# Stick-breaking attention: the causal mask of a diagonal block made by the running product

## The chip, the cores and the metric

The kernel runs on one core of one Trainium2 chip. The time is device microseconds of one execution, from three executions before the change. A core has five engines that run at the same time, each in the order of its own instructions: PE (matrix products; a product and the load of its stationary operand are two instructions), DVE (vector work), ACT (activations and copies), POOL (further vector work) and SP, which here only issues DMAs. Semaphores between them make one wait for another.

## What is computed

A decoder block over 2048 tokens of width 1024: a normalised and modulated input is projected to q, k, v (8 heads of 64) and to 4 pooling groups; attention and pooling are projected back, and a SwiGLU feed-forward of width 2816 follows. The part that matters is the attention. It is strictly causal, and the weight of key s for query t is a product of sigmoids:

```python
z = jnp.einsum('bhqd,bhkd->bhqk', qb, kb) * inv_sqrt
mask = s_idx < t_idx
log1m = jnp.where(mask, -jax.nn.softplus(z), 0.0)
after = lax.cumsum(log1m, axis=3, reverse=True) - log1m
logw = jax.nn.log_sigmoid(z) + after
w = jnp.where(mask, jnp.exp(jnp.where(mask, logw, 0.0)), 0.0)
outs.append(jnp.einsum('bhqk,bhkd->bhqd', w, vb))
```

So w[t, s] = sigmoid(z[t, s]) times the product over all s < j < t of sigmoid(-z[t, j]), and 0 for s >= t.

## The kernel before

The program has three stages: the projections (up to some 320 us), the attention (some 320 to 845 us), into which the rest of the projections is woven in small pieces, and the output projection with the feed-forward. In the first two the order of PE, ACT, DVE and POOL is the order in which the code is written; the order of SP's DMAs is set by a scheduler.

The attention works head by head. Tokens come in 4 blocks of 512 (`tb` for queries, `sc` for keys). A unit (`h, tb, sc`) is one block of queries against one block of keys, `sc` from `tb` down to 0, so the first unit of each `tb` is the diagonal one; 8 heads have 80 units, 32 of them diagonal. A unit is 4 steps, one for each 128 queries (`i`). A diagonal step needs only the first L = (i+1)*128 keys, any other all 512. There are 320 steps, 128 of them diagonal. The loop at L960 issues for each step, in this order:

- `values_step` (L844): two products with the values for an earlier step; they add up in the one output bank `av`, which ACT copies out (L858) when a block of queries is through.
- `weights_step` (L794): two products q*k (L803, L804), high and low half of q, into one of two score banks. In a diagonal step a third product (L806), identity times `neg_r`, adds -1e30 to the last 128 columns wherever the key is not before the query. Then ACT makes `sg` = sigmoid(z/8) (L808) and `pr` = sigmoid(-z/8) (L810).
- `scan_step` (L813), one step later: DVE's running product along `pr`, from the last key to the first (L821). It starts from 1 (`one`) in a diagonal unit and from the carry of the block to the right otherwise. The scan takes a second operand, which the operation `bypass` ignores: a bank of zeros, `idle` (L892). POOL sets the column after the last key to the start value (L818 or L820), keeps the carry (L825) and makes w = sg * pr shifted by one (L827).
- `turn_step` (L830), 7 steps later: four transposes of w on PE (L838), then the rounded copy `wth` on ACT (L59) and the rest `wtl` on DVE (L60), for `values_step`.
- pieces of the remaining projections: per piece three products (L69 to L71).

With -1e30 in z the masked `sg` are 0 and the masked `pr` are 1, so they add nothing and leave the running product alone. Keys, queries and values of a block are loaded by SP (L785 to L787) when their buffers come free; SP also stores the attention output (L860) and the pooled means (L389).

The constants of this part are made at the start: `ident_r` on DVE, `neg32` on POOL, `neg_r` on DVE (L159 to L171), `idle` just before the first attention step (L893).

Of the kernel before, what the change touches and what calls it, by code (L numbers as in the profile page):

```python
# [9 lines left out]
F32 = mybir.dt.float32  # L10
F32R = mybir.dt.float32r
AF = mybir.ActivationFunctionType
ALU = mybir.AluOpType
# [4 lines left out]
P = 128  # L18
# [10 lines left out]
TB = 512  # L29
NTB = S // TB  # L30
NT = S // P
EPS = 1e-6
NEG = -1e30
LAG = 2
OFF = 7
PRB = 6
# [8 lines left out]
def block_kernel(ctx, tc, x, c, w_cond, b_cond, g_mix_pre, g_mix_post, w_in, w_pool,  # L45
                 pool_scale, w_out, g_ffn_pre, g_ffn_post, w_gate, w_up, w_down, out):
    nc = tc.nc
# [25 lines left out]
    def open_pool(stack, name, bufs=1, side=None):  # L73
        kw = {"side": side} if side else {}
        return stack.enter_context(tc.tile_pool(name=name, bufs=bufs, reuse_waits="tile", **kw))
# [22 lines left out]
    ident = const.tile([P, P], F32, tag="ident", name="ident")  # L98
# [41 lines left out]
    c1 = open_pool(ph1, "c1")  # L140
# [3 lines left out]
    def psum(tag, bufs, name):  # L144
        return psp.tile([P, TB], F32, tag=tag, bufs=bufs, name=name)
# [7 lines left out]
    def bank_cycle(*tags):  # L153
        tags = itertools.cycle(tags)
        return lambda name: psum(next(tags), 1, name)

    z_ps, t_ps, av_ps, mm_only = bank_cycle("z0", "z1", "z2"), bank_cycle("w0", "w1"), bank_cycle("a0", "a1"), bank_cycle("mm")

    ident_r = c1.tile([P, P], F32R, tag="ident_r", name="ident_r")  # L159
    nc.vector.tensor_copy(ident_r, ident)  # L160
    ones = c1.tile([P, P], F32, tag="ones", name="ones")
    nc.vector.memset(ones, 1.0)
    one = ones[:, 0:1]
    ones_r = c1.tile([P, P], F32R, tag="ones_r", name="ones_r")
    nc.vector.tensor_copy(ones_r, ones)
    neg32 = c1.tile([P, P], F32, tag="neg32", name="neg32")
    nc.gpsimd.memset(neg32, 0.0)
    nc.gpsimd.affine_select(out=neg32, in_=neg32, compare_op=ALU.is_gt, fill=NEG, base=0,
                            pattern=[[-1, P]], channel_multiplier=1)
    neg_r = c1.tile([P, P], F32R, tag="neg_r", name="neg_r")  # L170
    nc.vector.tensor_copy(neg_r, neg32)  # L171
    rcnt = c1.tile([P, 16], F32, tag="rcnt", name="rcnt")
    for j in range(16):
        nc.gpsimd.memset(rcnt[:, j:j + 1], 1.0 / (j + 1))
# [239 lines left out]
    base = {"q": 0, "k": SBW, "u": 3 * SBW}  # L414
# [379 lines left out]
    def weights_step(u, i):  # L794

        h, tb, sc = u
        diag = sc == tb
        kt, qt = kv[h, sc][0], qts[h, tb]
        L = (i + 1) * P if diag else TB
        nm = f"{h}_{tb}_{sc}_{i}"  # L800
        z = z_ps(f"z{nm}")
        keys = kt[:, 0:L]
        nc.tensor.matmul(z[:, 0:L], qt[:, 0, i * P:(i + 1) * P], keys, start=True, stop=False)  # L803
        nc.tensor.matmul(z[:, 0:L], qt[:, 1, i * P:(i + 1) * P], keys, start=False, stop=not diag)  # L804
        if diag:
            nc.tensor.matmul(z[:, i * P:L], ident_r, neg_r, start=False, stop=True)  # L806
        sg = att.tile([P, TB], F32, tag="sg", bufs=5, name=f"sg{nm}")
        nc.scalar.activation(sg[:, 0:L], z[:, 0:L], AF.Sigmoid, scale=0.125)  # L808
        pr = att.tile([P, TB + 1], F32, tag="pr", bufs=PRB, name=f"pr{nm}")
        nc.scalar.activation(pr[:, 0:L], z[:, 0:L], AF.Sigmoid, scale=-0.125)  # L810
        scans.append((u, i, pr, sg, L, nm))

    def scan_step(u, i, pr, sg, L, nm):  # L813

        diag = u[1] == u[2]
        carry = carries.pop(i, None)
        if carry is None:
            nc.gpsimd.memset(pr[:, L:L + 1], 1.0)  # L818
        else:
            nc.gpsimd.tensor_copy(pr[:, L:L + 1], carry)  # L820
        nc.vector.tensor_tensor_scan(pr[:, 0:L][:, ::-1], pr[:, 0:L][:, ::-1], idle[:, 0:L],  # L821
                                     one if carry is None else carry, ALU.mult, ALU.bypass)
        if u[2]:
            carries[i] = att.tile([P, 1], F32, tag=f"carry{i}", bufs=2, name=f"carry{nm}")
            nc.gpsimd.tensor_copy(carries[i], pr[:, 0:1])  # L825
        w = att.tile([P, TB], F32, tag="w", bufs=OFF + 4, name=f"w{nm}")
        nc.gpsimd.tensor_tensor(w[:, 0:L], sg[:, 0:L], pr[:, 1:L + 1], ALU.mult)  # L827
        wss.setdefault(u, []).append(w)
# [43 lines left out]
    def fillers():  # L872
        yield from pieces(1, chunks, tasks, [first_filler])
        while small or urgent:
            run_small()
            yield
# [3 lines left out]
    fill = fillers()  # L880
# [8 lines left out]
        next(fill)  # L889
    taken = START  # L890
    attending = True
    idle = psum("z2", 1, "idle")  # L892
    nc.vector.memset(idle, 0.0)  # L893
    z_ps, t_ps, av_ps, mm_only = bank_cycle(*('z0', 'z1')), bank_cycle(*('w0', 'w1', 'a1')), bank_cycle(*('a0',)), bank_cycle(*('mm',))
    steps = [(u, i) for u in units for i in range(4)]

# [63 lines left out]
    for n in range(len(steps) + OFF):  # L960
        if len(waiting) > LAG:
            values_step(*waiting.pop(0))
        if n < len(steps):
            u, i = steps[n]
            if i == 0:
                unit_loads(u)
            weights_step(u, i)
            spent += 2.5 if u[1] == u[2] else 4.0
        if len(scans) > 1 or n >= len(steps) and scans:
            scan_step(*scans.pop(0))  # L970
# [4 lines left out]
        while fill is not None and taken < goal:  # L975
            taken += 1
            if next(fill, 0) == 0:
                fill = None
# [607 lines left out]
```

## Time and profile before

| | |
|---|---|
| median of 3 executions | 2335.81 us (2334.72 to 2337.44) |
| span of the profiled execution, first to last instruction | 2331.9 us |
| median time less that span | 3.9 us |
| instructions in the profile | 33384 |
| granted TensorE clock, mean | 0.992 |
| HBM read, written | 274.51 MB, 128.45 MB |

The profile gives busy time for each engine, the chain of work that ended last, groups of equal instructions, waits between engines, and the instructions in order of time. An instruction shows its source line, engine, operation, and out<-in by the program's names. PE's products overlap and their ends are modelled: how long PE is taken by one is read from the start of the next, not from its duration. Times of the profiled execution are set against its span; the 3.9 us around it are not part of the profile.

### The profile page before, as it was taken

How to read it: one execution, taken by the hardware profiler on the slowest of the kernel's cores; microseconds unless marked ns; L12 is line 12 of the kernel's file. 1: busy time of each engine (PE TensorE's matmuls, PEld its weight loads, DVE VectorE, ACT ScalarE, POOL GpSimd, SP SyncE). 2: the span in 40 equal slices, each digit the busy share in tenths (PEclk: the TensorE clock that was granted, in tenths of full speed). 3: DMA queues.
4: the chain of work that ended last, by engine and by line, in shares of the span. 5: the costliest groups of instructions: out<-in, count | busy, mean ns of one | idle time of the engine just before them, and what ended most of it. 6: DMA issues, size and time to landing. Idle time of an engine off the chain costs nothing.

```text
span 2331.9 us, 33384 instructions
## 1 busy us (share of the span) xinstructions
PE 2265.3 (97%) x10717; PEld 1861.7 (80%) x10717; DVE 1633.5 (70%) x2222; ACT 1165.0 (50%) x2411; POOL 1316.0 (56%) x1621
## 2 busy tenths in 40 slices
PE   6999999999999999999999999999999999999997
PEld 3777888788888778887888888788888888888885
DVE  6774559999999966756666665887766556565556
ACT  4323658889989854444323232554533323234444
POOL 4542347787778854555687878331486665641004
PEclk9999999999999999999999999999999999999998
DMA  8785764333435536655545455776753333328554
GB/s 287 258 293 186 289 179 116 110 100 94 124 105 152 166 105 207 215 196 177 172 154 160 156 158 185 266 244 217 256 177 117 110 113 91 113 90 281 193 194 145
DMA packets 307116, 405.17 MB, mean 174 GB/s; under 512 B 19254, under 2 KB 179578, under 8 KB 303868
## 3 DMA queue, kind: packets, MB, share of 16 engines
q1 hardware_dynamic: 302620, 400.68, 53.1%
q10 hardware_dynamic: 4320, 2.36, 0.4%
q8 instruction: 84, 1.38, 0.2%
q14 instruction: 92, 0.75, 0.1%
HBM read 274.51 MB, written 128.45 MB: 173 GB/s over the span
## 4 chain that ended last, share of the span: by engine, by line
PE 80%; DVE 5%; POOL 5%; issue 4%; DMA 3%; ACT 3%; SPq 1%; POOLq 0%; DVEq 0%; ACTq 0%
PE wt L838 4%; PE t_u L71 3%; PE t_u L69 3%; PE t_u L70 3%; PE t_g L70 3%; PE t_g L69 3%; PE t_g L71 3%; PE dn0p L70 3%; PE dn0p L71 3%; PE dn0p L69 3%; PE dn1p L70 3%; PE dn1p L69 3%; PE dn1p L71 3%; PE av L853 3%; PE av L854 2%
## 5 line engine op out<-in xcount | busy, mean ns | idle before, releaser
L827 POOL TENSOR_TENSOR w<-sg,pr 128x512 f32<-128x512 f32 (+2 forms) x320 | 307.3, 960 | 41.9 <-DVE pr L821 22.3
L1186 POOL TENSOR_TENSOR s<-s,cu 128x512 f32<-128x512 f32 x88 | 133.6, 1525 | 239.5 <-DVE cu L1185 130.9
L821 DVE TENSOR_TENSOR_SCAN pr<-pr,carry,idle 128x512 f32<-128x512 f32 x192 | 243.8, 1270 | 0.0
L808 ACT ACTIVATE sg<-z 128x512 f32<-128x512 f32 (+2 forms) x320 | 181.3, 567 | 56.4 <-PE z L806 25.8
L60 DVE TENSOR_TENSOR wtl<-wt,wth 128x512 fp32r<-128x512 f32 (+1 forms) x320 | 189.2, 592 | 27.0 <-ACT wth L59 25.2
L59 ACT CAST wth<-wt 128x512 fp32r<-128x512 f32 (+1 forms) x320 | 180.8, 566 | 12.7 <-PE wt L838 12.7
L810 ACT ACTIVATE pr<-z 128x512 f32<-128x512 f32 (+2 forms) x320 | 180.8, 565 | 0.0
L838 PE MATMUL wt<-ident,w 128*128 128x128 f32 x1088 | 173.7, 274 | 3.7 <-POOL w L827 1.9
L60 DVE TENSOR_TENSOR u_s_l<-u_s,u_s_h 128x512 fp32r<-128x512 f32 x66 | 67.3, 1020 | 153.1 <-ACT u_s_h L59 153.1
L838 PEld LDWEIGHTS wt<-ident,w 128*128 128x128 f32 x1088 | 129.3, 141 | 31.0 <-POOL w L827 2.6
L1176 ACT ACTIVATE s<-s 128x512 f32<-128x512 f32 x88 | 55.7, 633 | 192.9 <-DVE s L1175 192.9
L853 PE MATMUL av<-wth,vt 128*128 128x512 f32 (+1 forms) x320 | 129.3, 404 | 5.8 <-ACT o L858 5.8
L70 PE MATMUL dn0p<-w0p_l,g0p_h 128*128 128x512 f32 x308 | 121.1, 393 | 0.9 <-DVE w0p_l L60 0.9
L69 PE MATMUL dn0p<-w0p_h,g0p_h 128*128 128x512 f32 x308 | 120.5, 391 | 0.0
L71 PE MATMUL dn0p<-w0p_h,g0p_l 128*128 128x512 f32 x308 | 120.4, 391 | 0.0
L854 PE MATMUL av<-wtl,vt 128*128 128x512 f32 (+1 forms) x320 | 118.8, 371 | 1.6 <-DVE wtl L60 1.3
L803 PE MATMUL z<-kt,qt 128*128 128x512 f32 (+2 forms) x320 | 117.9, 368 | 2.1 <-ACT pr L810 1.3
L59 ACT CAST g_s_h<-g_s 128x512 fp32r<-128x512 f32 x66 | 39.5, 620 | 159.3 <-POOL g_s L1118 83.2
L60 DVE TENSOR_TENSOR u_a_l<-u,u_a_h 128x512 fp32r<-128x512 f32 x66 | 75.9, 1151 | 61.1 <-ACT u_a_h L59 61.1
L804 PE MATMUL z<-kt,qt 128*128 128x512 f32 (+2 forms) x320 | 117.1, 366 | 0.0
L59 ACT CAST u_s_h<-u_s 128x512 fp32r<-128x512 f32 x66 | 38.6, 614 | 153.2 <-POOL u_s L1118 153.2
L70 PE MATMUL dn1p<-w1p_l,g1p_h 128*128 128x512 f32 x292 | 114.4, 392 | 0.0
(656 smaller groups left out, 7297.3 us busy)
## 6 DMA issues: line engine op xcount, KB each, us to landing
g<-in_w_gate_dram SPq DMA_DIRECT2D x42, 512.0 KB, 4.7
u<-in_w_up_dram SPq DMA_DIRECT2D x42, 512.0 KB, 4.7
wc<-in_w_cond_dram SPq DMA_DIRECT2D x32, 512.0 KB, 5.8
qt<-qd SPq DMA_DIRECT2D x64, 256.0 KB, 3.9
wd<-in_w_down_dram SPq DMA_DIRECT2D x44, 256.0 KB, 2.9
tdt<-wd SPq DMA_DIRECT2D x44, 256.0 KB, 2.0
w0p<-tdt SPq DMA_DIRECT2D x44, 256.0 KB, 4.2
w1p<-tdt SPq DMA_DIRECT2D x44, 256.0 KB, 2.7
```

What stands on the lines that cost most here:

```text
L59: nc.scalar.copy(hi, src)
L60: low.tensor_tensor(lo, src, raw(hi), ALU.subtract)
L69: nc.tensor.matmul(ps, lh, rh, start=first and i == 0, stop=False)
L70: nc.tensor.matmul(ps, lh, rl, start=False, stop=False)
L71: nc.tensor.matmul(ps, ll, rh, start=False, stop=last and i == n - 1)
L808: nc.scalar.activation(sg[:, 0:L], z[:, 0:L], AF.Sigmoid, scale=0.125)
L810: nc.scalar.activation(pr[:, 0:L], z[:, 0:L], AF.Sigmoid, scale=-0.125)
L821: nc.vector.tensor_tensor_scan(pr[:, 0:L][:, ::-1], pr[:, 0:L][:, ::-1], idle[:, 0:L], one if carry is None else carry, ALU.mult, ALU.bypass)
L827: nc.gpsimd.tensor_tensor(w[:, 0:L], sg[:, 0:L], pr[:, 1:L + 1], ALU.mult)
L838: nc.tensor.transpose(wt[:, i * P:(i + 1) * P], wss[u][i][:, b * P:(b + 1) * P], ident)
L853: nc.tensor.matmul(av[:, lo0:], vb, wh[:, lo0:], start=first, stop=False)
L854: nc.tensor.matmul(av[:, lo0:], vb, wl[:, lo0:], start=False, stop=last)
```

## The change

The product that adds -1e30 is taken out, and with it its two operands. The scan of a diagonal step now has a maximum as its second operation, with a new operand `begin`: zeros, and an identity in the last 128 columns. The running product starts from 0 and stays 0 over the keys after the query; at the query's own position the maximum with 1 lifts it to 1, and from there it is the product as before. The masked weights are 0 because the shifted `pr` is 0 there. `begin` lies in the bank that held `idle`, all scans read it backwards, and those off the diagonal still ignore it.

```diff
-    ident_r = c1.tile([P, P], F32R, tag="ident_r", name="ident_r")
-    nc.vector.tensor_copy(ident_r, ident)
     ones = c1.tile([P, P], F32, tag="ones", name="ones")
     nc.vector.memset(ones, 1.0)
-    one = ones[:, 0:1]
...
-    neg32 = c1.tile([P, P], F32, tag="neg32", name="neg32")
-    nc.gpsimd.memset(neg32, 0.0)
-    nc.gpsimd.affine_select(out=neg32, in_=neg32, compare_op=ALU.is_gt, fill=NEG, base=0,
-                            pattern=[[-1, P]], channel_multiplier=1)
-    neg_r = c1.tile([P, P], F32R, tag="neg_r", name="neg_r")
-    nc.vector.tensor_copy(neg_r, neg32)
+    zero = c1.tile([P, 1], F32, tag="zero", name="zero")
+    nc.vector.memset(zero, 0.0)
...
-        nc.tensor.matmul(z[:, 0:L], qt[:, 1, i * P:(i + 1) * P], keys, start=False, stop=not diag)
-        if diag:
-            nc.tensor.matmul(z[:, i * P:L], ident_r, neg_r, start=False, stop=True)
+        nc.tensor.matmul(z[:, 0:L], qt[:, 1, i * P:(i + 1) * P], keys, start=False, stop=True)
...
-            nc.gpsimd.memset(pr[:, L:L + 1], 1.0)
+            nc.gpsimd.memset(pr[:, L:L + 1], 0.0)
...
-        nc.vector.tensor_tensor_scan(pr[:, 0:L][:, ::-1], pr[:, 0:L][:, ::-1], idle[:, 0:L],
-                                     one if carry is None else carry, ALU.mult, ALU.bypass)
+        nc.vector.tensor_tensor_scan(pr[:, 0:L][:, ::-1], pr[:, 0:L][:, ::-1], begin[:, TB - L:][:, ::-1],
+                                     zero if carry is None else carry, ALU.mult, ALU.max if diag else ALU.bypass)
...
-    idle = psum("z2", 1, "idle")
-    nc.vector.memset(idle, 0.0)
+    begin = psum("z2", 1, "begin")
+    nc.vector.memset(begin[:, 0:TB - P], 0.0)
+    nc.vector.tensor_copy(begin[:, TB - P:], ident)
```

The order of PE's instructions at one diagonal step, the last of the diagonal unit `tb` = 2 of the fifth head (512 keys), before (in a name the head's number is left out: `z_2_2_3` is query block 2, key block 2, step 3):

```order
L854 MATMUL av_1_7357<-wtl_1_1_1_7324,vt_1_7079 128x384
L803 MATMUL z_2_2_3_7382<-kt_2_7299,qt_2_7301 128x512
L804 MATMUL z_2_2_3_7382<-kt_2_7299,qt_2_7301 128x512
L806 MATMUL z_2_2_3_7382<-neg_r,ident_r 128x128
L838 MATMUL wt_1_0_0_7396<-ident,w_1_0_0_7238 128x128
L838 MATMUL wt_1_0_0_7396<-ident,w_1_0_1_7259 128x128
```

The same place of PE's order after (line numbers are lower by 8 to 10 here):

```order
L844 MATMUL av_1_7277<-wtl_1_1_1_7245,vt_1_7005 128x384
L795 MATMUL z_2_2_3_7301<-kt_2_7221,qt_2_7223 128x512
L796 MATMUL z_2_2_3_7301<-kt_2_7221,qt_2_7223 128x512
L828 MATMUL wt_1_0_0_7314<-ident,w_1_0_0_7160 128x128
L828 MATMUL wt_1_0_0_7314<-ident,w_1_0_1_7181 128x128
```

The mask product is gone from between the scores and the transposes; everything else stands as it did, here and at the other 127 diagonal steps.

The code says nothing of SP, but the scheduler puts a few of its DMAs elsewhere. The latest of these places in the attention stage, SP's order before (`kt_3_10842` are the keys of the last head's last block, loaded in two halves; `um` is a pooled mean, `o` an attention output):

```order
L786 DMA kt_3_10842<-kd_3_91 64x512
L860 DMA mtd_98<-o_6_2_10026 64x512
L860 DMA mld_102<-o_6_2_10026 64x512
L786 DMA kt_3_10842<-kd_3_91 64x512
L389 DMA mtd_98<-um_2_9763 128x512
L787 DMA vt_2_10534<-vd_94 128x4x128
```

And SP's order after, at the same place:

```order
L850 DMA mtd_98<-o_6_2_9908 64x512
L850 DMA mld_102<-o_6_2_9908 64x512
L778 DMA kt_3_10712<-kd_3_91 64x512
L381 DMA mtd_98<-um_2_9649 128x512
L778 DMA kt_3_10712<-kd_3_91 64x512
L779 DMA vt_2_10408<-vd_94 128x4x128
```

Both halves of the keys moved: the first behind the two stores of `o`, the second behind the store of the pooled mean. Four earlier places move a half load of keys or queries in the same way, by one to three rows.

More of the change, by code (lines that the diff above doesn't have):

```diff
@@ L32 @@
 EPS = 1e-6
-NEG = -1e30
 LAG = 2
```

## The prediction

> **What bounds the kernel now.** I read the page first, then busy time by stage, then the attention stage alone, because every edit that repeats lies there. The page's engine line and chain line:
>
> ```profile
> span 2331.9 us, 33384 instructions
> PE 2265.3 (97%) x10717; PEld 1861.7 (80%) x10717; DVE 1633.5 (70%) x2222; ACT 1165.0 (50%) x2411; POOL 1316.0 (56%) x1621
> ...
> PE 80%; DVE 5%; POOL 5%; issue 4%; DMA 3%; ACT 3%; SPq 1%; POOLq 0%; DVEq 0%; ACTq 0%
> ```
>
> Over the whole span the matrix engine fills 97% and carries 80% of the chain. That average is not the attention stage. The first step there starts near 320 us and the last ends near 845 us; busy time in that stretch:
>
> ```profile
> core 0: us, PE busy (x) PEld busy (x) DVE busy (x) ACT busy (x) POOL busy (x), PEclk, DMA share, GB/s
> 320.00:845.00 525.00, 511.75 (x2961) 429.44 (x2960) 502.93 (x649) 465.67 (x1057) 417.48 (x907) 1.00 0.43 122
> ```
>
> Here PE is at 511.75 of 525 us and DVE at 502.93 (96%): two engines are nearly full together, at a granted clock of 1.00. DVE's idle time is 525 - 502.93 = 22.1 us, and whatever this stage gains has to come out of that. The longest waits between engines in the stretch (total us, times, longest):
>
> ```profile
> ACT sg L808 <- PE z L806: 25.8, 46, 2.5
> ...
> DVE wtl L60 <- ACT wth L59: 19.0, 36, 1.3
> ACT sg L808 <- PE z L804: 16.7, 42, 0.8
> PEld av L853 <- ACT o L858: 12.5, 23, 1.2
> ```
>
> DVE waits for one thing only, 36 times: the rounded copy wth that ACT makes. ACT is late with it when it stands at sg, one place ahead in its queue, waiting for the scores z from PE. In 46 of 128 diagonal steps the product that releases sg is the very one the change removes (L806). So PE still leads part of this stage, through ACT to DVE, and DVE leads the rest.
>
> **The change, part by part.** *The 128 mask products go.* One for each of 8 heads, 4 diagonal blocks and 4 query rows:
>
> ```profile
> L806 PE MATMUL z<-neg_r,ident_r x128: 222/224/278, 319.6 to 816.1; 128*128 128x128 f32 x128
> ```
>
> The 224 ns are no price: ends are modelled and products overlap. The price is the time from its start to the start of the next product. Three places in the timeline, with 128, 256 and 512 keys:
>
> ```profile
> 811.47 0.28 PE L804 MATMUL z<-kt,qt 128*128 128x128 f32 x1
> 811.58 0.28 PE L806 MATMUL z<-neg_r,ident_r 128*128 128x128 f32 x1
> 811.69 0.62 PE L838 MATMUL wt<-ident,w 128*128 128x128 f32 x4
> ...
> 812.61 0.22 PE L806 MATMUL z<-neg_r,ident_r 128*128 128x128 f32 x1
> 812.67 0.51 PE L838 MATMUL wt<-ident,w 128*128 128x128 f32 x3
> ```
>
> ```profile
> 600.60 0.39 PE L804 MATMUL z<-kt,qt 128*128 128x512 f32 x1
> 600.83 0.22 PE L806 MATMUL z<-neg_r,ident_r 128*128 128x128 f32 x1
> 600.88 0.60 PE L838 MATMUL wt<-ident,w 128*128 128x128 f32 x4
> ```
>
> With 128 keys it costs 0.11 us (811.58 to 811.69), with 256 it costs 0.06, with 512 it costs 0.05; I take 0.06 for all but the first. That is 32 x 0.11 + 96 x 0.06 = 9.3 us of PE's issue time. The product ahead keeps its own cost: L804 with 128 columns takes 0.11 us to the next start as it is.
>
> How much of the 9.3 us reaches the end? The low end by rows: only the 46 steps in which ACT stood waiting for L806, at 9.3 / 128 = 0.07 us each, 3.3 us. Nothing at all is possible where DVE leads, so 0 stays an end of the range. The high end: all 9.3, which DVE's 22.1 us of idle time could still take in. The chain in a short piece, 600 to 602.6 us, shows L806 with its full price:
>
> ```profile
> by line: PE wt L838 21.2%; PE z L803 17.5%; PE z L804 15.7%; PE av L853 11.3%; PE av L854 11.1%; PE k L69 9.1%; PE k L70 8.8%; PE k L71 8.8%; PE z L806 4.7%
> ...
> 600.99 0.06 PE z L806
> ```
>
> 4.7% of 2.6 us is two times 0.06. But the chain favours PE: L804 above is given 0.39 us and the next product starts after 0.23, so the chain stays on PE whenever a release falls into the 0.16 us between. I therefore take a value between 3.3 and 9.3. The middle is 6.3; I take off 0.5 for the 23 places where PE waits for ACT to free the one output bank (the row PEld av L853 <- ACT o), since a lead that PE won before such a wait is passed on only if ACT is early too. **Term: -5.8 us.**
>
> *The stage behind* starts as much earlier. It runs on PE too (80% of the whole chain), none of its instructions change, so it passes the gain on.
>
> *The scans.* All 320 stay; the 128 diagonal ones take a real second operation (maximum) in place of bypass, and all read the second operand backwards. The trace holds no scan of that kind. The present ones, and the subtraction for comparison:
>
> ```profile
> L821 DVE TENSOR_TENSOR_SCAN pr<-pr,carry,idle 128x512 f32<-128x512 f32 x192 | 243.8, 1270 | 0.0
> L60 DVE TENSOR_TENSOR wtl<-wt,wth 128x512 fp32r<-128x512 f32 x218 | 146.6, 673 | 17.2 <-ACT wth L59 16.0
> L821 DVE TENSOR_TENSOR_SCAN pr<-pr,ones,idle 128x512 f32<-128x512 f32 x32 | 40.7, 1271 | 0.0
> ...
> L821 DVE TENSOR_TENSOR_SCAN pr<-pr,ones,idle 128x128 f32<-128x128 f32 x32 | 15.0, 470 | 0.0
> ...
> L60 DVE TENSOR_TENSOR wtl<-wt,wth 128x128 fp32r<-128x128 f32 x32 | 8.7, 271 | 2.6 <-ACT wth L59 2.2
> ```
>
> A scan takes (1271 - 470) / 384 = 2.09 ns an element, the subtraction (673 - 271) / 384 = 1.05. [...] For the maximum the nearest pair is one operation on one tensor against two operations on two:
>
> ```profile
> 14.32 0.48 DVE L213 TENSOR_SCALAR acc<-wcs,cs 128x512 f32<-128x512 f32 x1
> 14.83 0.75 DVE L215 SCALAR_TENSOR_TENSOR acc<-wcs,cs,acc 128x512 f32<-128x512 f32 x1
> ```
>
> That is 0.27 us on 512 elements, 0.53 ns an element; a gain I exclude, because bypass has nothing left to shorten. Ends: 0 and 0.53 ns. The diagonal scans cover 32 x (128 + 256 + 384 + 512) = 40,960 elements a partition, so 0 to 21.7 us. I take 0, being nearer in kind: these rows are scans, with their second operand already streamed. The other end is a rival below.
>
> *The setup.* ident_r, neg and neg_r are not made, one 128x1 zero is; before the first scan one fill of 512 becomes a fill of 384 and a copy of 128.
>
> ```profile
> 2.63 0.22 DVE L171 CAST neg_r<-neg 128x128 fp32r<-128x128 f32 x1
> ...
> 4.20 0.23 DVE L203 COPY colv<-tv 128x68 f32<-128x68 f32 x1 [1.27 <-PE tv L202]
> ```
>
> ```profile
> 317.06 0.48 DVE L893 MEMSET idle<- 128x512 f32 x1 [0.18 <-DVE k L60]
> 321.27 0.69 DVE L60 TENSOR_TENSOR k<-k,k 128x512 fp32r<-128x512 f32 x1 [3.72 <-ACT k L59]
> ```
>
> The cast of neg_r is over at 2.85 us and DVE then waits for a transposed load until 4.20; the fill is followed by 3.72 us of idle time, and a copy of 128 columns beside a cast of 0.22 us fits in. Both are 0; without those covers each would cost or save about 0.2 to 1 us, once.
>
> *The DMA queue.* The SP order shown above moves a few halves of key loads. The one that moves behind the latest store, kt for the last head's last block:
>
> ```profile
> 763.97 1.38 SPq L786 DMA_DIRECT2D kt<-kd  x1
> 767.71 0.33 SPq L389 DMA_DIRECT2D mtd<-um  x1
> ```
>
> Its second half will be issued some 4 us later, at about 768; its first readers are that block's first z products, those quoted above at 811.47. Some 43 us of cover, so 0; without the cover PE would lose those 4 us once.
>
> Sum: -5.8 + 0 + 0 + 0. Of the median 2335.81 the profiled span is 2331.9, so 3.9 us lie around it and are unchanged: span 2326.1, time **2330.0 us**.
>
> **The rivals.** *DVE leads the attention stage.* For it: 96% busy, and a PE whose shown ends are too late; PE stands waiting at its bank and at wtl. Against it: 46 + 42 waits of ACT for PE. Then only what is left of 3.3 us where DVE's stalls follow PE arrives, about half, 1.6 us: **2334.2**. [...]
>
> *PE leads everywhere.* For it: the chain. Then all 9.3 us arrive: **2326.5**.
>
> *The maximum lengthens the running product* (the other sign). At 0.53 ns an element DVE gets 21.7 us more work. It has 22.1 us idle, but in the diagonal blocks, where scans come one upon another, little of it; I let two thirds, 14.5 us, through after the PE gain has gone into it: **2350**. It decides from 5.8 us / 40,960 = 0.14 ns an element, 7% of the scan. Against it: the rows show a pace fixed at twice the subtraction's, whatever the length. [...] No run so far shows a maximum.
>
> That the change fails to remove the products is excluded: the list of PE's instructions falls from 10457 to 10329 rows, by 128.
>
> **How the numbers follow.** Forecast case 0.51, DVE leads 0.33, PE leads everywhere 0.09, longer scan 0.07. Faster or slower counts from 0.2%, 4.7 us, about what a measurement here can tell from no change (the three runs spread over 2.7 us). Faster: nine tenths of the forecast case and the whole of PE-everywhere, 0.55. Slower: the longer scan and a little of the scatter, 0.08. Same: the rest, 0.37. The range takes in the PE-everywhere price with its scatter at the low side and no gain plus scatter at the high side, 2326.0 to 2336.3; the long scan stays outside.
>
> **What would show it.** Right: the groups of L821's successor keep 1271 and 470 ns, the 128 mask rows are missing, the stretch from the first to the last attention step is 5 to 6 us shorter, DVE's idle time in it falls from 22 to about 16 us, and ACT's waits for z fall below 42 us. DVE leads: DVE idle stays near 20 us, and PE's waits for ACT and DVE grow by what was removed. Longer scan: the diagonal groups alone rise above 1271 and 470 ns while the 192 with a carry stay at 1270. Wrong altogether: a difference before 319 us or behind the attention stage, or a wait of PE for a key load.

## The result, and the profile after

| | before | changed |
|---|---|---|
| median, us (6 executions each) | 2335.26 (2333.65 to 2337.44) | 2326.99 (2323.79 to 2330.38) |
| ratio to before | | 0.9966, 95% interval 0.9954 to 0.9977 |
| span of the profiled execution | 2331.9 | 2328.3 |

The change makes the kernel 8.3 us faster, 5.4 to 10.7 us by the interval, whose near end (0.23%) just clears the bound of 0.2%. The forecast was 2330.0, 5.8 us; the range of 2326.0 to 2336.3 held, with 1.0 us to spare at its low end. The page of the changed kernel, engine line and chain:

```profile
span 2328.3 us, 33054 instructions
PE 2260.6 (97%) x10589; PEld 1854.3 (80%) x10589; DVE 1629.2 (70%) x2222; ACT 1163.5 (50%) x2411; POOL 1317.6 (57%) x1619
...
PE 81%; DVE 6%; DMA 4%; POOL 4%; issue 3%; ACT 2%; SPq 0%; POOLq 0%; DVEq 0%; ACTq 0%
```

PE has 128 instructions less, and its share does not move: averages over the span show nothing of an edit of 0.4%. The two spans are 3.6 us apart, the medians 8.3. So I measure by stages. The attention stage is taken from the start of the first q*k product to the start of the last product with the values (both read from the order of time). This is longer than the stretch to 845 us of the prediction: the last scans start near there, and the products with the values go on to 864.71. Busy time by engine in just that stretch, before:

```profile
319.43:864.71 545.28, 532.03 (x3061) 446.23 (x3059) 510.85 (x663) 472.84 (x1072) 422.62 (x913) 1.00 0.41 119
```

The same stretch of the changed kernel (columns as in the prediction: length, PE, weight loads, DVE, ACT, POOL, clock):

```profile
323.57:860.80 537.23, 522.95 (x2932) 433.90 (x2931) 509.37 (x663) 471.65 (x1072) 422.25 (x913) 1.00 0.43 121
```

The stage is 545.28 - 537.23 = 8.0 us shorter. DVE does the same work in it and is idle 27.9 us instead of 34.4. Behind it the two profiles agree (1467.2 and 1467.5 us to the end); ahead of it the changed kernel's profiled execution was 4.1 us later, which hides half the gain in the spans; what it goes with is told below, under the changed kernel again. PE at the place shown before, the last diagonal step of query block 2 of the fifth head:

```profile
600.03 0.40 PE L796 MATMUL z<-kt,qt 128*128 128x512 f32 x1
600.27 0.60 PE L828 MATMUL wt<-ident,w 128*128 128x128 f32 x4
```

From the second q*k product to the transposes it is 0.24 us now; before, 600.60 to 600.88, it was 0.28. The scans with the real maximum:

```profile
L811 DVE TENSOR_TENSOR_SCAN pr<-pr,carry,begin 128x512 f32<-128x512 f32 x192 | 244.4, 1273 | 0.0
...
L811 DVE TENSOR_TENSOR_SCAN pr<-pr,zero,begin 128x512 f32<-128x512 f32 x32 | 40.7, 1271 | 0.0
...
L811 DVE TENSOR_TENSOR_SCAN pr<-pr,zero,begin 128x128 f32<-128x128 f32 x32 | 15.1, 472 | 0.0
```

1271 and 472 ns against 1271 and 470: the maximum costs nothing that shows. The waits that ended the chain PE to ACT to DVE, before and then after, each in its own stretch:

```profile
ACT sg L808 <- PE z L806: 25.8, 46, 2.5
DVE wtl L60 <- ACT wth L59: 25.2, 40, 2.3
...
ACT sg L808 <- PE z L804: 16.7, 42, 0.8
```

```profile
ACT sg L798 <- PE z L796: 35.5, 76, 2.6
...
DVE wtl L59 <- ACT wth L58: 19.6, 34, 2.3
PEld av L843 <- ACT o L848: 13.7, 24, 1.2
```

ACT waits 35.5 us for scores where it waited 25.8 + 16.7 = 42.5; DVE's wait for `wth` fell by 5.6 us. The wait for the one output bank grew little: for the weight loads from 12.5 to 13.7 us, for the products themselves from 5.8 to 6.3. One more wait of PE before is gone after, in the third head, for a load of queries:

```profile
452.75 0.30 PE L803 MATMUL z<-kt,qt 128*128 128x128 f32 x1 [0.63 <-DMA qt<-qd]
```

So some 0.6 us of the 8.0 are not the product's issue time. The load's place in SP's order is the same in both kernels, and why it came in time after the change was not tested.

### The profile page after: what moved, and what is told of

Its sections match the earlier page's. It is cut to its first block, busy times and chain, and to the rows that moved or that the text cites. A ratio compares the mean times of both kernels' runs of the same rounds, so it can differ in the third digit from the quotient of the medians.

```text
span 2328.3 us, 33054 instructions
## 1 busy us (share of the span) xinstructions
PE 2260.6 (97%) x10589; PEld 1854.3 (80%) x10589; DVE 1629.2 (70%) x2222; ACT 1163.5 (50%) x2411; POOL 1317.6 (57%) x1619
## 4 chain that ended last, share of the span: by engine, by line
PE 81%; DVE 6%; DMA 4%; POOL 4%; issue 3%; ACT 2%; SPq 0%; POOLq 0%; DVEq 0%; ACTq 0%
PE wt L828 4%; PE t_u L70 3%; PE t_u L68 3%; PE t_u L69 3%; PE t_g L69 3%; PE t_g L68 3%; PE t_g L70 3%; PE dn0p L69 3%; PE dn0p L70 3%; PE dn0p L68 3%; PE dn1p L69 3%; PE dn1p L68 3%; PE dn1p L70 3%; PE av L843 3%; PE av L844 2%
## 5 line engine op out<-in xcount | busy, mean ns | idle before, releaser
L811 DVE TENSOR_TENSOR_SCAN pr<-pr,carry,begin 128x512 f32<-128x512 f32 x192 | 244.4, 1273 | 0.0
L798 ACT ACTIVATE sg<-z 128x512 f32<-128x512 f32 (+2 forms) x320 | 182.0, 569 | 49.6 <-PE z L796 35.5
L828 PEld LDWEIGHTS wt<-ident,w 128*128 128x128 f32 x1088 | 134.8, 141 | 35.4 <-POOL pr L808 3.2
L68 PE MATMUL dn1p<-w1p_h,g1p_h 128*128 128x512 f32 x292 | 114.3, 392 | 0.0
```

What stands on the lines that cost most here:

```text
L68: nc.tensor.matmul(ps, lh, rh, start=first and i == 0, stop=False)
L828: nc.tensor.transpose(wt[:, i * P:(i + 1) * P], wss[u][i][:, b * P:(b + 1) * P], ident)
```

## The experiments

Three theories stood at the start. **1:** PE leads the attention stage nearly throughout, so almost all of the 9.3 us of issue time arrives. **2:** only the steps in which ACT stood on the mask product count, and the rest of the 8 us is scatter. **3:** the gain comes from the scan, the setup or a moved DMA. The stage length repeats well (545.28 and, with the scan edit alone, 544.99; 537.23 and 537.07 in two profiles of the changed kernel), so it decides where the whole time scatters by several us. It has one uncertain part, the last head, where the granted clock falls to 0.50 for 3.4 us in some profiles (from 819.3 us before, from 816.3 us in the changed kernel) and stays at 1.00 in others (with half the heads). "Heads" are the distances between the first q*k products of successive heads, counted 40 steps to a head.

### The mask product twice

```diff
-            nc.tensor.matmul(z[:, i * P:L], ident_r, neg_r, start=False, stop=True)
+            nc.tensor.matmul(z[:, i * P:L], ident_r, neg_r, start=False, stop=False)
+            nc.tensor.matmul(z[:, i * P:L], ident_r, neg_r, start=False, stop=True)
```

> The kernel before, with each mask product issued twice (the mask becomes -2e30). From the rows, a 128-column product behind a 128-column product takes 0.11 us to the next start, so 128 x 0.11 = 14.1 us of PE time are added. If PE leads the attention stage nearly throughout (theory 1), some 12 to 14 us arrive: 0.5 to 0.6% slower, about 8 heads x 1.6 us. If only the waits of ACT for the mask product count (theory 2), 46/128 to 0.62 of it: 5 to 9 us. If the gain came from the scan or the setup (theory 3), 0.

Measured: 2349.02 us against 2337.01, ratio 1.0053 (1.0040 to 1.0066); stage 556.08 us, +10.8. The timeline confirms the price of the added product, with 128 keys:

```profile
609.47 0.28 PE L806 MATMUL z<-neg_r,ident_r 128*128 128x128 f32 x1
609.58 0.28 PE L807 MATMUL z<-neg_r,ident_r 128*128 128x128 f32 x1
609.70 0.51 PE L839 MATMUL wt<-ident,w 128*128 128x128 f32 x3
```

Start to start, the mask products together take 24.1 us where they took 10.3, so 13.9 us were added and 10.8, 78%, arrive. The time agrees with theory 1 (12 to 14 expected); the stage lies between its 12 and the 9 of theory 2, and decides against theory 3. The last head took only 0.1 us more, and its granted clock differs (its stretch of 14 us before, then here):

```profile
812.00:826.00 14.00, 12.00 (x63) 9.44 (x62) 11.57 (x15) 9.69 (x22) 11.33 (x26) 0.88 0.39 113
812.00:826.00 14.00, 12.31 (x71) 9.68 (x71) 12.40 (x17) 13.34 (x31) 10.70 (x28) 1.00 0.98 337
```

In the seven heads ahead of it, at a clock of 1.00 in both, 12.1 us were added and 10.7 arrive, 89%, which is nearer to theory 1.

### The scan edit alone

```diff
-        ... idle[:, 0:L],
-                                     one if carry is None else carry, ALU.mult, ALU.bypass)
+        ... idle[:, TB - L:][:, ::-1],
+                                     one if carry is None else carry, ALU.mult, ALU.max if diag else ALU.bypass)
```

> The kernel before, mask products kept; the diagonal scans take a maximum with zeros in place of bypass, and all scans read that operand backwards. Theories 1 and 2: no change, within 2 us, and the scan groups stay at 1271 and 470 ns. Theory 3: some part of the 8 us gain shows here. Were the maximum dearer by 0.5 ns an element, the diagonal groups would show 270 ns more at 512 and the time some 15 us more.

Measured: 2336.16 us, ratio 0.9997 (0.9989 to 1.0006); stage 544.99 us; no head moved by over 0.1 us but the last (0.2).

```profile
L821 DVE TENSOR_TENSOR_SCAN pr<-pr,carry,idle x192: 1268/1272/1283, 334.7 to 847.6; 128x512 f32<-128x512 f32 x192
L821 DVE TENSOR_TENSOR_SCAN pr<-pr,ones,idle x128: 455/870/1282, 326.5 to 824.8; 128x128 f32<-128x128 f32 x32, 128x256 f32<-128x256 f32 x32, 128x384 f32<-128x384 f32 x32, 128x512 f32<-128x512 f32 x32
```

455 to 1282 ns where it was 455 to 1273. With the stage 0.3 us off, the maximum and the backward operand cost and bring nothing that shows. The scan's part of theory 3 falls.

### Half the heads

```diff
+        product = diag and h >= 4
...
-        if diag:
+        if product:
...
+                                     (one if u[0] >= 4 else zero) if carry is None else carry, ALU.mult,
+                                     ALU.max if diag and u[0] < 4 else ALU.bypass)
```

The setup makes the constants of both kernels.

> Heads 0 to 3 as in the changed kernel, heads 4 to 7 as before (mask product, start value 1, bypass). Theory 1: heads 0 to 3 are each about 1 us shorter than before, heads 4 to 7 as before, in all 4 us less. Theory 2: 0.7 us each in heads 0 to 3, in all 3 us less. If the gain is one thing that happens once (setup, the first stage, a DMA that moved), the per-head times don't follow the split.

Measured: 2327.39 us, ratio 0.9965 (0.9953 to 0.9977). By the time alone, half the edit would bring all of the gain. By stages it does not:

| stage, us less than before | head 1 | 2 | 3 | 4 | 5 | 6 | 7 | 8 and tail | sum |
|---|---|---|---|---|---|---|---|---|---|
| changed | 0.73 | 1.01 | 1.45 | 0.85 | 0.93 | 1.35 | 0.92 | 0.81 | 8.0 |
| half the heads | 0.76 | 1.04 | 1.38 | 1.01 | 0.03 | 0.05 | 0.03 | 1.11 | 5.4 |

The gain follows the split: 4.2 us in the four heads without the product, nothing in heads 5 to 7. That is theory 1, and no single event. Heads 3 and 6 gain more than the 1.2 us that their products took before; in head 3 it is the wait for the queries shown above, in head 6 it stays open. The 1.11 us of the last head, which kept its product, and some 4 us outside the attention stage go, in the profiled execution, with the granted clock. Two stretches, one at the end of the attention, one after the first output tiles (length, PE, weight loads, DVE, ACT, POOL, then the clock), before:

```profile
810.00:825.00 15.00, 12.13 (x66) 9.57 (x65) 12.57 (x18) 10.31 (x23) 12.92 (x26) 0.89 0.46 141
1050.00:1070.00 20.00, 15.50 (x60) 11.97 (x59) 11.90 (x17) 12.43 (x23) 7.29 (x5) 0.83 0.58 195
```

The same stretches with half the heads:

```profile
810.00:825.00 15.00, 12.22 (x65) 9.14 (x64) 13.65 (x19) 12.59 (x27) 12.26 (x30) 1.00 0.41 114
1050.00:1070.00 20.00, 17.16 (x77) 13.15 (x76) 17.14 (x23) 14.35 (x27) 7.69 (x6) 1.00 0.48 156
```

Where the clock fell to 0.89 and 0.83 before, this execution kept 1.00; the clock so lost, 0.11 x 15 + 0.17 x 20 = 5.0 us, is an estimate of what it can cost. Its mean clock over the span is 0.995, against 0.987 to 0.993 in the 17 executions of before beside it. That is not the whole of the median, though: the executions with a mean clock of 0.990 or 0.991 average 2336.4 us before (10 of them), 2328.2 changed (5, from both measurements) and 2329.2 with half the heads (3, spread over 2.9 us). At an equal clock half the heads is still 7.2 us faster where its heads show 4.2. The median of this kernel is partly luck of five executions, and some 3 us of it stay open.

### The changed kernel again

> The changed kernel again, as it is. Its first profile shows the attention stage 8.0 us shorter and the stage ahead of it 4.1 us longer. If the 4.1 us belong to the change, this profile shows the first attention step at about 323.6 us again and the time is 4 us less than before; if they are scatter of that one execution, the first step is found anywhere from 318 to 324 us and the time is about 8 us less than before.

Measured: 2326.82 us against 2337.01, 10.2 us less, ratio 0.9959 (0.9947 to 0.9971); stage 537.07 us, 8.2 less than before. The time decides that the 4.1 us are no price of the change: 4 us less was expected if they were. The first q*k product starts at 322.6 us. In the other profiles it starts at 319.4 (before), 319.1 (half the heads), 324.1 (scan edit alone) and 325.4 (mask twice), so kernels with the old setup start both early and late. No profile without the old setup starts before 322.6. The start goes with the granted clock of the first 320 us: 0.98 in the two early profiles, 0.96 in the two of the changed kernel.

### More work for DVE

If PE leads, work given to another engine should vanish. The six kernels from here on were run once each (2328.1 us with the fill, 2328.6 and 2333.0 with the products, then 2328.8, 2338.7 and 2338.2), so only their stages are read. First, a fill of 128x16 ahead of each diagonal scan of the changed kernel:

```diff
+        if diag:
+            nc.vector.memset(extra, 0.0)
         nc.vector.tensor_tensor_scan(
```

> The changed kernel with a fill of 128x16 on DVE ahead of each of the 128 diagonal scans. The fill of mhalf (128x1) took 0.06 us, so some 8 to 10 us of DVE time. The attention stage (first q*k product to last product with the values) is 537.1 us in the changed kernel. If PE leads and DVE has slack (theory 1), it grows by less than 3 us; if DVE leads as much as PE, by 6 us or more.

Measured: stage 537.68 us, 0.4 to 0.6 more than the changed kernel. It settles nothing, because the fill lies beside the scan:

```profile
599.03 0.46 DVE L814 TENSOR_TENSOR_SCAN pr<-pr,zero,begin 128x128 f32<-128x128 f32 x1
599.04 0.07 DVE L813 MEMSET extra<- 128x16 f32 x1
599.40 0.40 DVE L59 TENSOR_TENSOR wtl<-wt,wth 128x256 fp32r<-128x256 f32 x1
```

From the scan to the next instruction it is 0.37 us with the fill in between, no more than the 0.39 us without it. A product in the fill's place, 16 and then 64 columns wide:

```diff
+        if diag:
+            nc.vector.tensor_tensor(extra, ones[:, 0:16], begin[:, 0:16], ALU.mult)
```

> The fill of the run before lay beside the scan (its start is 10 to 20 ns after the scan's) and cost DVE next to nothing, so it settled nothing. Here a product of 128x16 with a PSUM operand stands ahead of each diagonal scan in the changed kernel. Reading off the subtractions (271 ns at 128 elements, 1.05 ns an element, 80 ns of overlap with the next) it should take DVE 0.07 to 0.1 us each, 9 to 13 us. If PE leads and DVE has slack, under a third arrives and the stage stays below 541 us; if DVE leads as much as PE, 6 us or more arrive, 543 us or more.

> The same with 128x64: 0.05 us more each, 15 to 20 us of DVE time in all, against 27.9 us that DVE is idle in the changed kernel's stage. With slack on DVE the stage grows by 3 to 8 us, more than with 128x16 in proportion, because the slack runs out; if DVE leads, by 12 us or more.

```profile
600.75 0.16 DVE L813 TENSOR_TENSOR extra<-ones,begin 128x16 f32<-128x16 f32 x1
600.82 0.47 DVE L814 TENSOR_TENSOR_SCAN pr<-pr,zero,begin 128x128 f32<-128x128 f32 x1
```

This one takes 0.077 us to the next start, 9.8 us in 128 steps; with 64 columns 0.127 us, 16.2 us. The stage grew by 1.3 us (538.53) and by 5.0 us (542.21). The first of these looks better than it is, because its last head had the clock at 1.00 where the changed kernel's fell (the stretch of the changed kernel, then of this one):

```profile
812.00:826.00 14.00, 11.12 (x53) 8.73 (x52) 11.77 (x15) 10.62 (x23) 10.63 (x27) 0.88 0.41 112
812.00:826.00 14.00, 11.69 (x63) 8.71 (x61) 12.75 (x20) 11.08 (x24) 11.84 (x27) 1.00 0.38 112
```

In the seven heads ahead of it 2.0 of 8.6 us arrive, 23%, and with 64 columns 4.4 of 14.2 us, 31%. So DVE, 95% busy, has slack behind PE, but not a store of it that work vanishes into: nearly a quarter arrives from the start, and more as the work grows.

### More work for ACT

```diff
+        if diag:
+            nc.scalar.copy(extra, ones[:, 0:16])
         nc.scalar.activation(sg[:, 0:L], z[:, 0:L], AF.Sigmoid, scale=0.125)
```

> The changed kernel with a copy of 128x16 on ACT ahead of each of the 128 diagonal sg. Copies of 128x16 on ACT stand 0.115 us apart in the profile before, so some 15 us of ACT time. Theory 1: ACT has slack but stands between PE and DVE, so less than a third arrives, under 5 us. If ACT belongs to what leads the stage, 10 us or more.

The copies stand about 0.11 us ahead of the next start, 14 us in all. ACT's busy time in the stage rose from 471.7 to 482.1 us, 10.4; the stage grew by 2.0 us (539.18), a fifth of that or less. ACT has slack too.

### More work for PE, off the diagonal

```diff
-        nc.tensor.matmul(z[:, 0:L], qt[:, 1, i * P:(i + 1) * P], keys, start=False, stop=True)
+        nc.tensor.matmul(z[:, 0:L], qt[:, 1, i * P:(i + 1) * P], keys, start=False, stop=diag)
+        if not diag:
+            nc.tensor.matmul(z[:, L - P:L], ident_r, zero_r, start=False, stop=True)
```

The setup makes `ident_r` and `zero_r`, which is zeros.

> The changed kernel with a 128-column product of the identity and zeros in each of the 192 steps off the diagonal, where there was none. At 0.06 us each behind a 512-column product, 11.5 us of PE time. If PE leads the whole stage, 9 us or more arrive; if PE leads only in the diagonal units and DVE elsewhere (a step off the diagonal has 1.19 + 0.58 = 1.77 us on DVE), under 4 us.

```profile
608.01 0.22 PE L804 MATMUL z<-zero_r,ident_r 128*128 128x128 f32 x1
608.08 0.60 PE L836 MATMUL wt<-ident,w 128*128 128x128 f32 x4
```

192 such products take 11.8 us start to start, and the stage grew by 8.1 us (545.37): 69% arrive, and in the first seven heads 73%, three times the 23% of a like dose on DVE. PE leads off the diagonal as well, though less than in the mask products' own steps.

### Two output banks

PE still waited for the one output bank, so the changed kernel was tried with two, taking one from the transposes:

```diff
-... bank_cycle(*('w0', 'w1', 'a1')), bank_cycle(*('a0',)), ...
+... bank_cycle(*('w0', 'w1')), bank_cycle(*('a0', 'a1')), ...
```

> The changed kernel with two output banks (a0, a1) and two banks for the transposes instead of one and three. In the changed kernel PE or its weight load waits 36 times, 20 us, for ACT to copy the one output bank. If those waits are what PE loses, the stage gets up to 10 us shorter than 537.1; if two banks are too few for the transposes, PE waits there for DVE and ACT instead, and the stage is as long or longer.

Measured: stage 550.71 us, 13.5 longer. The wait for the bank is gone and another has taken its place:

```profile
PEld wt L828 <- DVE wtl L59: 33.7, 65, 2.2
...
PE wt L828 <- DVE wtl L59: 15.3, 45, 1.8
```

With two banks PE waits 65 times until DVE has read the transposes. None of the kernels tried is faster than the changed one beyond what scatter allows.

## Why the prediction came out as it did

- **The price of a mask product** (0.05 to 0.11 us, 9.3 us in all) was right: the old kernel's products stand 10.3 us from their next starts, waits included, and doubling them added what the rows said.
- **How much of it arrives** is the term that was mis-sized. I took 5.8 of 9.3 us, 62%; the stage shows 8.0 and 8.2, 87%. The step that failed is "the chain favours PE", with the discount drawn from it: the middle of 3.3 and 9.3 was taken where the measured value lies near the high end. The 0.5 us for PE's wait at the output bank fits what was seen (5.8 to 6.3 us). The 3.3 us low end had counted only the steps in which ACT visibly stood on the mask product, but most of a product's time arrived in the other steps too, as the products off the diagonal show. Of the 8.0 us some 0.6 are the wait for the queries in the third head, which no term of the sum had. The range held because its low end was set by the rival's price, not by the forecast's own mechanism. The chain, followed piece by piece, has the mask product in it 109 times, 8.2 us together. The first of those pieces, and the last:

```profile
319.76 0.11 PE z L806
...
794.43 0.08 PE z L806
```

That sum would have been the better forecast. With the product twice the chain has the mask products in it 222 times, 20.6 us: 12.4 us more, where the stage grew by 10.8. That the chain is exact on PE does not follow from these two cases.
- **DVE leads** (2334.2, chance 0.33) fell: of work added to it 23 to 31% arrives, of work added to PE 69 to 89%. The busy shares of the stage before, 94% for DVE and 98% for PE, do not show that distance; the added work does.
- **PE leads everywhere** (2326.5, chance 0.09) came nearest in time. It is not the whole truth: 69 to 89% of a product's time arrives, not all.
- **The longer scan** fell with 1271 and 472 ns in the changed kernel, and with 455 to 1282 ns in the scan edit alone, where it was 455 to 1273. With a maximum the pace is (1271 - 472) / 384 = 2.08 ns an element, against 2.09 before. What sets this pace no run shows: the 0 for the maximum and the backward operand was the author's estimate, and the runs showed 472 and 1271 ns at 128 and 512 elements against 470 and 1271.
- **Setup and the DMA queue** at 0: the first stage scatters by some 6 us, so a gain or loss under that cannot be read from it. In the attention stage of the changed kernel PE waits for no load at all; the one such wait before, 0.63 us for queries, is gone. The half-changed kernel does not part the two causes, because the scheduler moved its DMAs only in the four heads that were changed; so for moved loads it rests on the waits.
- **The 3.9 us around the span** were not all around it. The changed kernel's profiled execution took 2330.08 us for a span of 2328.3, so 1.8 us lie around it; the rest was that the profile before was of a faster execution than the median. The difference forecast is untouched.
- **What was to be seen**: the stage 5 to 6 us shorter (8.0), DVE's idle time down by 6 us (6.5 over the longer stretch), ACT's waits for scores under 42 us (35.5).

## What to carry to other kernels

Two engines at 97 and 95% need not lead together: which of them leads shows when a known dose of work is put on one and then the other, and here 10 us on DVE cost some 2 while 12 on PE cost 8. Price a removed product by the distance to the next start, and look up how often the chain itself holds it before discounting the chain. Where the whole time scatters by 7 us, compare the length of the stage that the edit touches and the parts of it that the edit does not, and look at the granted clock of each part first.

## What the runs showed of the hardware that was not expected

- A small fill on DVE (72 ns) ran beside a scan in progress and cost nothing that shows (0.37 us from the scan to the next start, 0.39 without it), while a small product of two operands ahead of the scan cost 0.077 us.
- The granted clock was 0.50 from 819.3 to 822.7 us and from 1058.2 to 1065.0 us of the profile before, the second time from within a wait of PE of 4.50 us that ended at 1059.22 us, and 0.99 to 1.00 beside it. With half the heads it was 1.00 in both places. In the stage the difference is of the order of 1 us in the last head (1.11 us with half the heads). The start of the attention goes with the clock of the first 320 us (0.98 at 319.1 and 319.4 us, 0.96 at 322.6 and 323.6).
